# The second matmul of a matmul–GELU–matmul kernel from seven half-size products

## The chip, the cores and the metric

The kernel runs on one core of a Trainium2 chip. The metric is the device time of one execution in microseconds, as a median over several executions. Beside these, one execution was profiled, and its trace gives the start and end of each instruction.

## The reference

```python
m, k, n, p = 1024, 1024, 2048, 1024        # a: m x k, b: k x n, c: n x p, all float32
h = np.matmul(a, b)
h = 0.5 * h * (1 + np.tanh(np.sqrt(2 / np.pi) * (h + 0.044715 * h ** 3)))
return np.matmul(h, c).astype(np.float32)
```

Two matmuls, with a tanh GELU between them. Each has 1024 x 1024 x 2048 multiply-adds.

## The kernel before

The output of the first matmul is kept transposed in SBUF: `hT[h]` holds n on the partitions (16 tiles of 128, the index `t`) and 512 of the 1024 rows of a in the free dimension; `h` is 0 for the upper and 1 for the lower half of a's rows. So the first matmul takes tiles of b as weights and a transposed, `aT[h]` (8 tiles of k), as moving operand; the second takes tiles of `hT[h]` as weights and rows of c as moving operand. All operands of TensorE are bf16. A matmul instruction has 128 x 128 weights and up to 512 moving columns[...]. Six banks rotate in the pool `ppool`, two in `tpool`.

The order of the work is written by hand, and each engine works through its instructions in the order of the program:

1. SP loads the upper half of a and 768 columns of b (six tiles `t`) in pieces by k. VectorE casts a (L91), TensorE transposes it (L94), VectorE copies it out (L95), ScalarE casts b (L97), and TensorE runs six tiles for each k (`mm0`, L86).
2. A small GpSimd copy (L75) waits for a piece of b. Behind it GpSimd issues, in its order, all other loads, which cast float32 to bf16 on the way: 512 columns of b in four DMAs of two k tiles each (L110, called from L115), 768 columns of b in four DMAs of four k tiles (L134), the lower half of a in four blocks of 128 rows (L142), and c in eight DMAs of two row tiles each (L137). The program waits for an older DMA of its eight slots before it issues a new one.
3. TensorE runs tiles 6 to 9 of the upper half k by k (L118), and then tiles 10 to 15 one after another (`mm1`, L127). After each of the tiles 11 to 14 it transposes one block of the lower half of a (`turn`, L149), and VectorE copies that into `aT[1]` (L150).
4. `mm1` runs all 16 tiles of the lower half. ScalarE applies the GELU to each bank (L103).
5. The second matmul: for each of eight row tiles and two halves of the columns, 16 steps add up in one bank (L171), VectorE copies the bank to SBUF (L163), and SP stores it (L164). The last 512 columns are done as two pieces of 256.

Of the kernel before, what the change touches and what calls it, by code (L numbers as in the profile page):

```python
# [8 lines left out]

F32 = mybir.dt.float32  # L10
BF16 = mybir.dt.bfloat16
AF = mybir.ActivationFunctionType
PSUM = bass.MemoryType.PSUM


@with_exitstack
def kernel(ctx, tc, a, b, c, out):
    nc = tc.nc
    M, K = a.shape
    _, N = b.shape  # L20
    _, P = c.shape
    KT = K // 128
    NT = N // 128
    MT = M // 128
    H = 512
    N0 = 6
    W0 = N0 * 128
    N1 = 4
    W1 = N1 * 128

    av = a.rearrange("(mt p) k -> p mt k", p=128)
    bv = b.rearrange("(kt p) n -> p kt n", p=128)
    cv = c.rearrange("(nt p) q -> p nt q", p=128)

    ctx.enter_context(tc.manual_schedule())
    consts = ctx.enter_context(tc.tile_pool(name="consts", bufs=1))
    keep = ctx.enter_context(tc.tile_pool(name="keep", bufs=1))
    astage = ctx.enter_context(tc.tile_pool(name="astage", bufs=4))
    abf = ctx.enter_context(tc.tile_pool(name="abf", bufs=4))
    b0stage = ctx.enter_context(tc.tile_pool(name="b0stage", bufs=8))  # L40
    opool = ctx.enter_context(tc.tile_pool(name="opool", bufs=4))
    ppool = ctx.enter_context(tc.tile_pool(name="ppool", bufs=6, space=PSUM))
    tpool = ctx.enter_context(tc.tile_pool(name="tpool", bufs=2, space=PSUM))

    warm = consts.tile([128, H], BF16, name="warm")
    nc.vector.memset(warm, 0.0)  # L46
    ident = consts.tile([128, 128], BF16, name="ident")
    make_identity(nc, ident)

    aT = [keep.tile([128, KT, H], BF16, name=f"aT{h}") for h in range(2)]  # L50
    b_sb = keep.tile([128, KT, N], BF16, name="b_sb")
    c_sb = keep.tile([128, NT, P], BF16, name="c_sb")
    hT = [keep.tile([128, NT, H], BF16, name=f"hT{h}") for h in range(2)]


    a_st, b_st = {}, {}

    def load_a0(k, n):
        st = astage.tile([128, 4, 256], F32, name="a_st")
        nc.sync.dma_start(out=st[:, :, 0:n * 128], in_=av[:, 0:4, ds(k * 128, n * 128)])  # L60
        for i in range(n):
            a_st[k + i] = st[:, :, ts(i, 128)]

    def load_b0(k):
        st = b0stage.tile([128, W0], F32, name="b0_st")
        nc.sync.dma_start(out=st, in_=bv[:, k, 0:W0])  # L66
        b_st[k] = st

    gate = consts.tile([128, 1], F32, name="gate")
    for k, n in ((0, 1), (1, 1), (2, 2), (4, 2), (6, 2)):  # L70
        load_a0(k, n)
        for i in range(n):
            load_b0(k + i)

    nc.gpsimd.tensor_copy(gate, b_st[5][:, 0:1])  # L75
    g = consts.tile([128, 1], F32, name="g")
    nc.scalar.activation(g, warm[:, 0:1], AF.Gelu_apprx_tanh)
    wps = tpool.tile([128, H], F32, name="pt")
    for _ in range(10):
        nc.tensor.matmul(wps, warm[:, 0:128], warm, start=True, stop=True)  # L80

    ps = [ppool.tile([128, H], F32, name="ps") for _ in range(N0)]

    def mm0(k):
        for t in range(N0):
            nc.tensor.matmul(ps[t], b_sb[:, k, ts(t, 128)], aT[0][:, k, :],  # L86
                             start=(k == 0), stop=(k == KT - 1))

    for k in range(KT):
        ab = abf.tile([128, 4, 128], BF16, name="ab")  # L90
        nc.vector.tensor_copy(ab, a_st[k])  # L91
        pt = tpool.tile([128, H], BF16, name="pt")
        for j in range(4):
            nc.tensor.transpose(pt[:, ts(j, 128)], ab[:, j, :], ident)  # L94
        nc.vector.tensor_copy(aT[0][:, k, :], pt)  # L95
        for i in range(2):
            nc.scalar.activation(b_sb[:, k, ts(i, W0 // 2)], b_st[k][:, ts(i, W0 // 2)], AF.Copy)  # L97
        if k > 0:
            mm0(k - 1)
    mm0(KT - 1)  # L100

    def gelu(t, h, p):
        nc.scalar.activation(hT[h][:, t, :], p, AF.Gelu_apprx_tanh)  # L103

    for t in range(N0):
        gelu(t, 0, ps[t])


    def load_b(k0, kn, n0, w):
        nc.gpsimd.dma_start(out=b_sb[:, k0:k0 + kn, ds(n0, w)], in_=bv[:, k0:k0 + kn, ds(n0, w)])  # L110

    ps = [(tpool if t < 2 else ppool).tile([128, H], F32, name="pt" if t < 2 else "ps")
          for t in range(N1)]
    for k in range(0, KT, 2):
        load_b(k, 2, W0, W1)  # L115
        for i in range(2):
            for t in range(N1):
                nc.tensor.matmul(ps[t], b_sb[:, k + i, ds(W0 + t * 128, 128)], aT[0][:, k + i, :],  # L118
                                 start=(k + i == 0), stop=(k + i == KT - 1))
    for t in range(N1):  # L120
        gelu(N0 + t, 0, ps[t])


    def mm1(t, h):
        p = ppool.tile([128, H], F32, name="ps")
        for k in range(KT):
            nc.tensor.matmul(p, b_sb[:, k, ts(t, 128)], aT[h][:, k, :],  # L127
                             start=(k == 0), stop=(k == KT - 1))
        gelu(t, h, p)

    W2 = 384
    for n0 in range(W0 + W1, N, W2):
        for k in range(0, KT, 4):
            load_b(k, 4, n0, W2)  # L134

    def load_c(t0):
        nc.gpsimd.dma_start(out=c_sb[:, t0:t0 + 2, :], in_=cv[:, t0:t0 + 2, :])  # L137

    a1 = []
    for j in range(4):  # L140
        st = abf.tile([128, K], BF16, name="ab1")
        nc.gpsimd.dma_start(out=st, in_=av[:, 4 + j, :])  # L142
        a1.append(st)

    def turn(j):
        ab = a1[j]
        pt = tpool.tile([128, KT, 128], BF16, name="pt")
        for k in range(KT):
            nc.tensor.transpose(pt[:, k, :], ab[:, ts(k, 128)], ident)  # L149
        nc.vector.tensor_copy(aT[1][:, :, ts(j, 128)], pt)  # L150

    for t in range(N0 + N1, NT):
        mm1(t, 0)
        if NT - 5 <= t < NT - 1:
            turn(t - (NT - 5))
    for t in range(0, NT, 2):
        load_c(t)
    for t in range(NT):
        mm1(t, 1)

    def store(mt, q0, w, p):
        ot = opool.tile([128, H], F32, name="ot")
        nc.vector.tensor_copy(ot[:, 0:w], p)  # L163
        nc.sync.dma_start(out=out[ts(mt, 128), ds(q0, w)], in_=ot[:, 0:w])  # L164

    for mt in range(MT):
        h, j = divmod(mt, 4)
        for q0, w in ((0, 512), (512, 512)) if mt < MT - 1 else ((0, 512), (512, 256), (768, 256)):
            p = ppool.tile([128, w], F32, name="ps", padded_shape=[128, H])
            for t in range(NT):  # L170
                nc.tensor.matmul(p, hT[h][:, t, ts(j, 128)], c_sb[:, t, ds(q0, w)],  # L171
                                 start=(t == 0), stop=(t == NT - 1))
            store(mt, q0, w, p)


# [1 line left out]
_INS = ['a', 'b', 'c']  # L177
# [26 lines left out]
```

## Time and profile before

| | us |
|---|---|
| median of 11 runs | 131.39 |
| lowest and highest run | 130.78, 133.93 |
| the profiled execution, its own time | 132.36 |
| its span in the trace | 130.3 |
| TensorE busy, share of the span | 119.8, 92% |
| VectorE busy | 20.9, 16% |
| ScalarE busy | 27.2, 21% |
| second matmul (L171) in the chain that ended last | 55.31, from 71.60 |

The span goes from the first to the last instruction in the trace. The rest of the profiled execution's time, 2.06 us, lies around it. TensorE's granted clock was 0.996 of full speed. "PE" is TensorE's matmul, "PEld" its weight load, which runs beside matmuls, "DVE" VectorE, "ACT" ScalarE, "POOL" GpSimd and "SP" the engine that issues plain DMAs. An instruction is named by its line, its engine, its operation and its tiles, output first (`ps<-c_sb,hT`). "Idle before" is the time in which the engine stood still just ahead of such an instruction, followed by what ended it. The chain that ended last follows the work back from the last instruction, at each step to what released it.

### The profile page before, as it was taken

Reading aid. Unit: us, or ns where it says so; the run is one execution under the profiler, and the core shown is the slowest. Engines: PE = TensorE matmul, PEld = TensorE weight load, DVE = VectorE, ACT = ScalarE, POOL = GpSimd, SP = SyncE. Lnnn points to the kernel's source line nnn. Section 1 sums busy time; section 2 is a strip of 40 time slices with the busy share of each in tenths; the row PEclk is TensorE's granted clock in tenths of the full one; section 3 lists DMA queues with packets and bytes.
Section 4 is the critical chain, followed back from the end, with each engine's and each line's share of the span. In section 5 each row is a group of like instructions: output and inputs, shape, how many; then the busy total and the mean of one; then the engine's idle time right before and its main releaser. Section 6 shows DMA issues by size and latency. Waiting matters only on the chain.

```text
span 130.3 us, 1431 instructions
## 1 busy us (share of the span) xinstructions
PE 119.8 (92%) x602; PEld 56.4 (43%) x602; DVE 20.9 (16%) x38; ACT 27.2 (21%) x50; POOL 14.6 (11%) x27
## 2 busy tenths in 40 slices
PE   6847899999299999999999999999999999999990
PEld 2324444443156444444444444444444444444570
DVE  0224451000042100000000022222222222221121
ACT  4055556426113233333333100000000000000000
POOL 2000198333452000000000000000000000000000
PEclk9999999999999999999999999999999999999998
DMA  3999999999999999960000022222111122222231
GB/s 109 212 358 377 379 259 153 190 202 206 210 210 210 211 212 210 211 114 2 0 0 5 0 81 81 81 81 80 62 55 63 67 81 81 81 81 81 81 121 40
DMA packets 12196, 17.37 MB, mean 133 GB/s; under 512 B 800, under 2 KB 6688, under 8 KB 12192
## 3 DMA queue, kind: packets, MB, share of 16 engines
q0 software_dynamic: 5952, 7.87, 35.1%
q1 hardware_dynamic: 6240, 9.44, 20.8%
q8 instruction: 4, 0.07, 0.2%
HBM read 20.97 MB, written 4.19 MB: 193 GB/s over the span
## 4 chain that ended last, share of the span: by engine, by line
PE 70%; DMA 17%; SPq 5%; POOL 5%; issue 0%; DVE 0%
PE ps L171 42%; PE ps L127 27%; DMA ab<-in_a_dram 10%; DMA b_st<-in_b_dram 7%; POOL b_sb L110 4%; SPq L66 3%; PE pt L149 2%; SPq L60 1%; DVE ot L163 0%; POOL gate L75 0%
## 5 line engine op out<-in xcount | busy, mean ns | idle before, releaser
L171 PE MATMUL ps<-c_sb,hT 128*128 128x512 bf16 (+1 forms) x272 | 55.5, 367 | 0.0
L171 PEld LDWEIGHTS <-hT 128*128 128x128 bf16 x272 | 26.6, 98 | 28.9
L127 PE MATMUL ps<-aT,b_sb 128*128 128x512 bf16 x176 | 38.9, 379 | 0.0
L127 PEld LDWEIGHTS <-b_sb 128*128 128x128 bf16 x176 | 17.0, 98 | 20.0 <-DMA b_sb<-in_b_dram 0.4
L103 ACT ACTIVATE hT<-ps 128x512 bf16<-128x512 f32 x30 | 17.3, 602 | 29.6 <-PE ps L127 28.4
L163 DVE COPY ot<-ps 128x512 f32<-128x512 f32 (+1 forms) x17 | 11.2, 661 | 73.2 <-PE ps L171 73.2
L86 PE MATMUL ps<-aT,b_sb 128*128 128x512 bf16 x48 | 11.5, 379 | 0.0
L97 ACT ACTIVATE b_sb<-b_st 128x384 bf16<-128x384 f32 x16 | 7.5, 515 | 10.4 <-DMA b_st<-in_b_dram 10.2
L94 PE MATMUL pt<-ident,ab 128*128 128x128 bf16 x32 | 3.4, 232 | 3.6 <-DVE ab L91 3.6
L137 POOL DMA_DIRECT2D c_sb<-in_c_dram x8 | 5.7, 714 | 7.5 <-DMA b_sb<-in_b_dram 5.3
L86 PEld LDWEIGHTS <-b_sb 128*128 128x128 bf16 x48 | 4.4, 98 | 4.0
L150 DVE COPY aT<-pt 128x1024 bf16<-128x1024 bf16 x4 | 2.8, 692 | 20.0 <-PE pt L149 20.0
L110 POOL DMA_DIRECT2D b_sb<-in_b_dram x8 | 6.0, 769 | 0.0
L80 PE MATMUL pt<-warm 128*128 128x512 bf16 x10 | 4.5, 632 | 1.2 <-DVE warm L46 1.2
L94 PEld LDWEIGHTS <-ab 128*128 128x128 bf16 x32 | 2.3, 104 | 6.6 <-DVE ab L91 5.6
L118 PEld LDWEIGHTS <-b_sb 128*128 128x128 bf16 x32 | 3.1, 98 | 3.8
L118 PE MATMUL pt<-aT,b_sb 128*128 128x512 bf16 x16 | 4.8, 379 | 0.0
L118 PE MATMUL ps<-aT,b_sb 128*128 128x512 bf16 x16 | 4.8, 379 | 0.0
L149 PE MATMUL pt<-ident,ab 128*128 128x128 bf16 x32 | 2.5, 219 | 2.3 <-DMA ab<-in_a_dram 2.3
L91 DVE CAST ab<-a_st 128x512 bf16<-128x512 f32 x8 | 3.5, 441 | 6.1 <-DMA a_st<-in_a_dram 6.1
L95 DVE COPY aT<-pt 128x512 bf16<-128x512 bf16 x8 | 3.4, 425 | 6.3 <-PE pt L94 6.3
L149 PEld LDWEIGHTS <-ab 128*128 128x128 bf16 x32 | 2.0, 98 | 3.5 <-DMA ab<-in_a_dram 2.8
(13 smaller groups left out, 7.4 us busy)
## 6 DMA issues: line engine op xcount, KB each, us to landing
c_sb<-in_c_dram POOLq DMA_DIRECT2D x8, 512.0 KB, 16.1
out_dram<-ot SPq DMA_DIRECT2D x15, 256.0 KB, 2.0
b_st<-in_b_dram SPq DMA_DIRECT2D x8, 384.0 KB, 8.3
a_st<-in_a_dram SPq DMA_DIRECT2D x3, 512.0 KB, 8.5
b_sb<-in_b_dram POOLq DMA_DIRECT2D x4, 384.0 KB, 11.0
b_sb<-in_b_dram POOLq DMA_DIRECT2D x4, 256.0 KB, 6.8
ab<-in_a_dram POOLq DMA_DIRECT2D x4, 256.0 KB, 12.8
a_st<-in_a_dram SPq DMA_DIRECT2D x2, 256.0 KB, 4.4
```

What stands on the lines that cost most here:

```text
L80: nc.tensor.matmul(wps, warm[:, 0:128], warm, start=True, stop=True)
L86: nc.tensor.matmul(ps[t], b_sb[:, k, ts(t, 128)], aT[0][:, k, :], start=(k == 0), stop=(k == KT - 1))
L94: nc.tensor.transpose(pt[:, ts(j, 128)], ab[:, j, :], ident)
L97: nc.scalar.activation(b_sb[:, k, ts(i, W0 // 2)], b_st[k][:, ts(i, W0 // 2)], AF.Copy)
L103: nc.scalar.activation(hT[h][:, t, :], p, AF.Gelu_apprx_tanh)
L110: nc.gpsimd.dma_start(out=b_sb[:, k0:k0 + kn, ds(n0, w)], in_=bv[:, k0:k0 + kn, ds(n0, w)])
L118: nc.tensor.matmul(ps[t], b_sb[:, k + i, ds(W0 + t * 128, 128)], aT[0][:, k + i, :], start=(k + i == 0), stop=(k + i == KT - 1))
L127: nc.tensor.matmul(p, b_sb[:, k, ts(t, 128)], aT[h][:, k, :], start=(k == 0), stop=(k == KT - 1))
L137: nc.gpsimd.dma_start(out=c_sb[:, t0:t0 + 2, :], in_=cv[:, t0:t0 + 2, :])
L149: nc.tensor.transpose(pt[:, k, :], ab[:, ts(k, 128)], ident)
L163: nc.vector.tensor_copy(ot[:, 0:w], p)
L171: nc.tensor.matmul(p, hT[h][:, t, ts(j, 128)], c_sb[:, t, ds(q0, w)], start=(t == 0), stop=(t == NT - 1))
```

## The change

The second matmul is cut in halves in all three dimensions: h into h11, h12 (rows of the upper half; n in 0..1023 and 1024..2047), h21 and h22 (rows of the lower half), and c into c11, c12, c21, c22. The four quarters of the output are made from seven products of these halves in place of eight, with sums formed ahead of the products (operand sums) and behind them:

- operand sums: s1 = h21 + h22, s2 = s1 - h11, s3 = h11 - h21, s4 = h12 - s2; t1 = c12 - c11, t2 = c22 - t1, t3 = c22 - c12, t4 = t2 - c21
- products, in TensorE's order: h11·c11; h12·c21 (three of its four row tiles); s2·t2; s3·t3; s1·t1; s4·c22; h22·t4; and last the fourth row tile of h12·c21, in two pieces of 256 columns

h11, h12, c11, c12 and c21 stay in bf16. h21, h22, c22 and all operand sums are float32r (4 bytes), and so five of the products have float32r operands on both sides. All sums run on VectorE (`tensor_tensor`), 44 on operands, and one or two for each product bank, in place of its copies to the output tile; banks of the first product are copied out by ScalarE. GpSimd copies one bank's result aside for the last piece.

c is loaded by quarters, in the order c11, c22, c21, c12, each in two DMAs of four row tiles. Several tiles take the place of others: c12 and then half of s2 that of `aT[0]`, the other half of s2 that of `aT[1]`, t3 and u3 those of the two parts of b, t1 and t2 the staging tiles of the start. The operand sums are written into the program between and behind the tiles of the lower half, in the order t1, t2, then s1 and t3 by turns, s2, s3. s4 stands between the banks of s3·t3, t4 between those of s1·t1.

In the first half the transposes of a's lower half move: block 0 behind tile 13, blocks 1 to 3 behind tile 14, before tile 15. The 512 columns of b for tiles 6 to 9 are loaded in two DMAs of four k tiles in place of four of two.

```diff
-    b_sb = keep.tile([128, KT, N], BF16, name="b_sb")
-    c_sb = keep.tile([128, NT, P], BF16, name="c_sb")
-    hT = [keep.tile([128, NT, H], BF16, name=f"hT{h}") for h in range(2)]
+    b_lo = keep.tile([128, KT, WB], BF16, name="b_lo", tag="B0")
+    b_hi = keep.tile([128, KT, N - WB], BF16, name="b_hi", tag="B1")
+    hq = [[keep.tile([128, NH, H], F32R if h else BF16, name=f"h{h}{g}") for g in range(2)]
+          for h in range(2)]
...
-    for k in range(0, KT, 2):
-        load_b(k, 2, W0, W1)
-        for i in range(2):
+    for k in range(0, KT, 4):
+        load_b(k, 4, W0, W1)
+        for i in range(4):
...
-        if NT - 5 <= t < NT - 1:
-            turn(t - (NT - 5))
-    for t in range(0, NT, 2):
-        load_c(t)
+        if t == NT - 3:
+            turn(0)
+        if t == NT - 2:
+            turn(1)
+            turn(2)
+            turn(3)
...
+    def load_c(dst, r, q):
+        for t in range(0, NH, 4):
+            nc.gpsimd.dma_start(out=dst[:, t:t + 4, :], in_=cv[:, r * NH + t:r * NH + t + 4, ts(q, H)])
+    load_c(c11, 0, 0)
+    load_c(c22, 1, 1)
+    load_c(c21, 1, 0)
+    load_c(c12, 0, 1)
...
     for t in range(NT):
         mm1(t, 1)
+        if 3 <= t < 7:
+            sum_t1(t - 3)
+        if 6 <= t < 10:
+            sum_t2(2 * (t - 6))
+            sum_t2(2 * (t - 6) + 1)
+        if t == WB // 128:
+            t3 = keep.tile([128, NH, H], F32R, name="t3", tag="B0")
+        if t >= NH + 1:
+            sum_s1(t - NH - 1)
+        if WB // 128 <= t < WB // 128 + 4:
+            i = t - WB // 128
+            nc.vector.tensor_tensor(t3[:, ts(i, 2), :], c22[:, ts(i, 2), :], c12[:, ts(i, 2), :], op=SUB)
+    sum_s1(NH - 1)
+    for i in range(4):
+        nc.vector.tensor_tensor(pair(s2, i), s1[:, ts(i, 2), :], h11[:, ts(i, 2), :], op=SUB)
+    for i in range(4):
+        nc.vector.tensor_tensor(h21[:, ts(i, 2), :], h11[:, ts(i, 2), :], h21[:, ts(i, 2), :], op=SUB)
+    s3 = h21
...
+    def prod(p, lhs, rhs, j, q=slice(0, H)):
+        for t in range(NH):
+            nc.tensor.matmul(p, lhs(t)[:, ts(j, 128)], rhs(t)[:, q],
+                             start=(t == 0), stop=(t == NH - 1))
+    def combine(m, q, p, u, op=ADD, swap=False):
+        ot = new_out()
+        nc.vector.tensor_tensor(ot, u if swap else p, p if swap else u, op=op)
+        store(ot, m, q * H)
...
+    for j in R:
+        p = bank()
+        prod(p, whole(h11), whole(c11), j)
+        nc.scalar.activation(u2[j], p, AF.Copy)
+    for j in range(3):
+        p = bank()
+        prod(p, whole(h12), whole(c21), j)
+        combine(j, 0, p, u2[j])
+    last = u2[3]
+    last_keep = opool.tile([128, H], F32, name="lk", bufs=1)
+    nc.gpsimd.tensor_copy(last_keep, last)
+    for j in R:
+        p = bank()
+        prod(p, halves(s2), ones(t2), j)
+        nc.vector.tensor_tensor(u2[j], p, u2[j], op=ADD)
+    for j in R:
+        p = bank()
+        prod(p, whole(s3), whole(t3), j)
+        nc.vector.tensor_tensor(u3[:, j, :], p, u2[j], op=ADD)
+        sum_s4(j)
+    for j in R:
+        p = bank()
+        prod(p, whole(s1), pairs(t1), j)
+        combine(4 + j, 1, p, u3[:, j, :])
+        nc.vector.tensor_tensor(u2[j], p, u2[j], op=ADD)
+        sum_t4(2 * j)
+        sum_t4(2 * j + 1)
+    for j in R:
+        p = bank()
+        prod(p, halves(s2), whole(c22), j)
+        combine(j, 1, p, u2[j])
+    for j in R:
+        p = bank()
+        prod(p, whole(h22), ones(t2), j)
+        combine(4 + j, 0, p, u3[:, j, :], op=SUB, swap=True)
+    for q in range(2):
+        w = H // 2
+        p = bank(w)
+        prod(p, whole(h12), whole(c21), 3, q=ds(q * w, w))
+        ot = new_out()
+        nc.vector.tensor_tensor(ot[:, 0:w], p, last_keep[:, ds(q * w, w)], op=ADD)
+        store(ot, 3, q * w, w)
```

## The prediction

> **What bounds the kernel now.** I read the page first (busy shares, then the chain of work that ended last), then that chain in order of time, then the groups by shape, and last the timelines of GpSimd, TensorE and VectorE around the first half.
>
> ```profile
> PE 119.8 (92%) x602; PEld 56.4 (43%) x602; DVE 20.9 (16%) x38; ACT 27.2 (21%) x50; POOL 14.6 (11%) x27
> ...
> PE ps L171 42%; PE ps L127 27%; DMA ab<-in_a_dram 10%; DMA b_st<-in_b_dram 7%; POOL b_sb L110 4%; SPq L66 3%; PE pt L149 2%; SPq L60 1%; DVE ot L163 0%; POOL gate L75 0%
> ```
>
> TensorE is the bound and VectorE is nearly free. The second matmul (L171) alone is 42% of the chain. In order of time:
>
> ```profile
> 71.60 55.31 PE ps L171 x272
> 126.91 0.02 issue
> 126.93 0.43 DVE ot L163
> ```
>
> From 71.60 to 126.91 TensorE waits for nothing. The 272 steps are 240 of 512 columns and 32 of 256, worth 256 full ones: 55.31 / 256 = 0.216 us each, start to start. [...] The span's last 3.4 us are the final eviction and store.
>
> Weight loads and evictions by shape (columns: number | busy, mean ns | idle before, who ended it):
>
> ```profile
> L171 PEld LDWEIGHTS <-hT 128*128 128x128 bf16 x272 | 26.6, 98 | 28.9
> L163 DVE COPY ot<-ps 128x512 f32<-128x512 f32 x15 | 10.4, 692 | 70.8 <-PE ps L171 70.8
> ```
>
> A bf16 weight load takes 98 ns and lies wholly beside the matmul before it. The only stall of TensorE in the middle is ahead of the first late transposes, 2.3 us for block 0 of a's lower half:
>
> ```profile
> 35.11 0.62 PE L149 MATMUL pt<-ident,ab 128*128 128x128 bf16 x8 [2.31 <-DMA ab<-in_a_dram]
> ```
>
> GpSimd's timeline dates the loads, since each later issue waits for an earlier load's slot:
>
> ```profile
> 21.82 0.60 POOL L142 DMA_DIRECT2D ab<-in_a_dram  x1
> 23.54 0.55 POOL L142 DMA_DIRECT2D ab<-in_a_dram  x1 [1.12 <-DMA b_sb<-in_b_dram]
> 24.83 0.53 POOL L142 DMA_DIRECT2D ab<-in_a_dram  x1 [0.75 <-DMA b_sb<-in_b_dram]
> 26.11 0.53 POOL L142 DMA_DIRECT2D ab<-in_a_dram  x1 [0.74 <-DMA b_sb<-in_b_dram]
> ```
>
> There are eight slots and eight loads of b ahead, so these waits end when b's loads 2, 3 and 4 (two k tiles each, for L118) land: 23.5, 24.8 and 26.1 us. By the same reading the four loads behind them land at 28.3, 30.3, 32.2 and 34.1 (issues of c at 28.27 to 34.10), and a's four blocks at 35.1, 36.7, 37.9 and 39.1. In one-microsecond windows the load of c fades out at 57.3 us:
>
> ```profile
> 56.00:57.00 1.00, 1.00 (x7) 0.41 (x5) 0.00 (x0) 0.60 (x1) 0.00 (x0) 1.00 0.93 174
> 57.00:58.00 1.00, 1.00 (x6) 0.47 (x5) 0.00 (x0) 0.17 (x1) 0.00 (x0) 1.00 0.27 49
> ```
>
> (last column GB/s written; it was 211 until then).
>
> [...] No row of the trace has a 4-byte matmul. [...] The trace shows the bf16 load only. [...] The trace's bf16 stream, 128 x 512 x 2 bytes in 0.216 us, is 607 GB/s[...] and leaves open whether 4 bytes go as fast. [...] The trace's 512-column fp32 eviction takes 692, so I use 692[...].
>
> **The change, part by part.**
>
> *Product steps.* Seven products of 32 steps are 224 full steps in place of 256: 64 in bf16 (h11·c11, h12·c21, the last of them in halves) and 160 in float32r. The built program has one weight load and one matmul for each step[...]. Its step costs at least 0.216 us[...]. Above, there are two ends: the weight load isn't overlapped, +98 ns (the bf16 load's length, as a stand-in)[...]. I take 0.216: [...]a load twice as long as 98 ns still fits beside a 216 ns matmul. So 224 x 0.216 = 48.4 against 55.3: -6.9 us.
>
> *b for L118 in two loads, not four.* The first load now brings k 0 to 3, so it lands when load 2 did, 23.5. L118 began at 22.15. A new stall on the path, +1.4 us; lower end 0 (it lands before 22.15), upper end about 2. The next one (26.1) is needed at 23.55 + 16 x 0.216 = 27.0, in time. GpSimd issues two DMAs fewer ahead of a; the queue behind is full, so no landing moves.
>
> *Late transposes.* L118 ends at 23.55 + 6.9 = 30.45; tiles 10 to 13 (32 steps) end at 37.35, their b having landed by 34.1. Block 0 (35.1) is there: the 2.3 us stall is gone. Transposes 0.45 → 37.8; tile 14 → 39.55; blocks 1 and 2 → 40.45. Block 3 has landed (39.1), but there are two transpose banks, so it waits for block 1's copy: 40.0 + 0.2 + 0.69 = 40.9, → 41.35. Tile 15 → 43.1. Before, tile 15 began at 42.09 and ended at 43.8. Net of both edits: -0.7 us (-2.1 without the new stall). VectorE's copy of block 3 ends near 42.2, ahead of the second half.
>
> *Loads of c.* Same bytes, 2 KB rows for 4 KB, c22 written as 4 bytes; I cost it at nothing, as the queue reads at about 420 GB/s now (211 written as bf16). c12 takes the place of aT[0] and can't be issued before tile 15 ends (43.1); six of eight loads are ahead of it and run to about 54 (39.1 + 6.3 MB at 420), so GpSimd's wait is covered. Only c12 is queued behind it. c12 lands at 57.3.
>
> *Sums on VectorE.* t1, the first sum, needs c12, and all else queues behind it. After 57.3, up to the last t4 that product 7 needs: 18 of 1024 columns (two t1, four each t3, s2, s3, s4) x 1.224 = 22.0, and 43 of 512 (eight t2, eight s1, 19 operations on product banks, eight t4) x 0.692 = 29.8. Sum 51.8, so t4 ends at 109.1 if VectorE never rests. TensorE's second matmul starts at 70.9 (71.6 - 0.7); product 3 at 70.9 + 56 x 0.216 = 83.0, when s2 is ready at 57.3 + 23.3 = 80.6 (26 operations). Product 7 starts at 70.9 + 184 x 0.216 = 110.6. VectorE is ahead by 1.5 to 2.4 us: nothing on the path, but if that cover went, it would cost microsecond for microsecond. In its favour, two operations in a row overlap in the trace:
>
> ```profile
> 11.22 0.42 DVE L95 COPY aT<-pt 128x512 bf16<-128x512 bf16 x1 [0.49 <-PE pt L94]
> 11.56 0.42 DVE L91 CAST ab<-a_st 128x512 bf16<-128x512 f32 x1
> ```
>
> (0.34 apart, 0.42 long), which would give back up to 61 x 0.08 = 4.9 us. ScalarE's four copies (0.60 each, as L103) and GpSimd's copy of the kept bank have idle engines. Banks: product 3's fourth bank waits for the combine behind s3, 0.3 us on the path, my allowance (0 to 1).
>
> *Sum.* 130.3 - 6.9 - 0.7 + 0.3 = 123.0 us span. The profiled execution took 132.36 with 2.06 outside its span: 125.1. The median of the runs is 131.39, 0.9927 of it: **124.1 us**.
>
> **Rivals.**
> - *VectorE becomes the bound.* If an operation costs 80 ns more than its length instead of less, s2 is 2.1 late and t4 4.9, less the 1.5 to 2.4 in hand: +3.0, 127.1 us. For it: 61 operations without rest, many depending on the one before. Against: the overlap above.
> - *The wider load is hidden.* The first load of b lands before 22.15: -1.4, 122.7 us. For it: fewer issues. Against: load 2 landed at 23.5.
> - *float32r is somewhat slower,* +25 ns a step: +4.0, 128.1 us.
> - *Slower than before: the 4-byte weight load isn't hidden.* Place: 160 steps of products 3 to 7. At +98 ns, 15.7 us: 139.7 us[...]. It decides from 7.3 / 160 = 46 ns a step. For it: [...]no 4-byte row in the trace. Against: TensorE's loads are only 98 of each 216 ns.
>
> **How the numbers follow.** Forecast 0.50; VectorE bound 0.17; load hidden 0.11; somewhat slower float32r 0.06 (0.03 faster, 0.02 same, 0.01 slower); weight load exposed 0.16. A measurement tells about 0.3% from no change. Faster 0.81, same 0.02, slower 0.17. The range 121.8 to 128.2 takes in the first three and most of the fourth, 0.82; only the two ends of the float32r price are left out. The likeliest case's own range is 122.7 to 125.6.
>
> **What would show it.** Right: float32r matmuls 0.216 apart; a stall of about 1.4 us ahead of L118's first step, none ahead of block 0's transposes; the second matmul some 48.5 us long; VectorE busy almost without a break from 57 to 109, TensorE hardly waiting for it. Wrong: a float32r spacing over 0.26; TensorE's waits for VectorE adding to over 2 us; c12 landing after 60.

## The result and the profile after

| | before | after |
|---|---|---|
| median, us | 131.73 (47 runs) | 124.83 (12 runs, 124.33 to 125.62) |
| the profiled execution, us | 132.36 | 124.74 |
| its span, us | 130.3 | 123.0 |

The ratio of the runs is 0.950, with a 95% interval of 0.947 to 0.952; it leaves out executions in a slower state, which the kernel before shows in some of its runs, and so it is not the quotient of the two medians. The forecast was 124.1, with a range of 121.8 to 128.2, and a span of 123.0. The span agrees to the tenth, but, as the steps below show, because errors cancelled.

The page of the changed kernel, busy shares and then the chain that ended last:

```profile
PE 115.2 (94%) x562; PEld 67.2 (55%) x562; DVE 65.1 (53%) x94; ACT 29.6 (24%) x54; POOL 21.6 (18%) x26
...
PE ps L246 41%; PE ps L143 31%; DMA a_st<-in_a_dram 12%; PE ps L102 3%; PE ps L134 3%; PE pt L134 3%; PE pt L162 1%; DVE aT L163 1%; PE pt L110 1%; DVE ab L107 0%; SPq L82 0%; DVE ot L316 0%; SPq L76 0%; DVEq L107 0%
```

There are 40 steps fewer on TensorE and three times the work on VectorE, and still VectorE is on the chain with 1% only. The end of the same chain in order of time (start, length, what):

```profile
38.77 0.70 DVE aT L163
...
40.13 29.35 PE ps L143 x136
69.48 50.14 PE ps L246 x232
...
119.64 0.42 DVE ot L316
```

The second matmul starts at 69.48 where it was 71.60, and takes 50.14 us where it was 55.31. These two differences, 2.1 and 5.2, are the whole of the 7.3 us. The 0.70 us of VectorE is the copy of block 1, for whose bank the transposes of block 3 wait. TensorE's timeline shows the second matmul product by product (the chain counts its start 0.16 us behind the first step's own, in the kernel before as here):

```profile
69.32 12.25 PE L246 MATMUL ps<-c,h 128*128 128x512 bf16 x56
81.22 7.62 PE L246 MATMUL ps<-t,s 128*128 128x512 f32 x32
88.67 7.42 PE L246 MATMUL ps<-t,h 128*128 128x512 f32 x32
95.92 7.42 PE L246 MATMUL ps<-t,s 128*128 128x512 f32 x32
103.18 7.42 PE L246 MATMUL ps<-c,s 128*128 128x512 f32 x32
110.43 7.42 PE L246 MATMUL ps<-t,h 128*128 128x512 f32 x32
117.69 1.92 PE L246 MATMUL ps<-c,h 128*128 128x256 bf16 x16
```

No line has an idle time in brackets: TensorE waits for no sum. Take the starts, not the lengths (a bf16 matmul of 512 columns is 379 ns long in the table of groups): from 88.67 to 117.69 are 128 float32r steps, 226.7 ns each, where bf16 steps stand 216 apart. (The first float32r step is recorded at 81.22, though 56 bf16 steps of 216 ns from 69.32 end at 81.42. So I count back from 88.67.) VectorE's timeline has the sums that TensorE needs; the lines are the first sums of t1, then s2, s3 and the combines behind it, and the last sums of t4:

```profile
56.52 2.36 DVE L200 TENSOR_TENSOR t<-c,c 128x1024 fp32r<-128x1024 bf16 x2 [15.66 <-DMA c<-in_c_dram]
...
75.56 4.63 DVE L230 TENSOR_TENSOR s<-s,h 128x1024 fp32r<-128x1024 f32 x4
80.10 4.63 DVE L232 TENSOR_TENSOR h<-h,h 128x1024 fp32r<-128x1024 bf16 x4
84.64 1.89 DVE L269 TENSOR_TENSOR ot<-ps,u 128x512 f32<-128x512 f32 x3
...
106.34 1.29 DVE L239 TENSOR_TENSOR t<-t,c 128x512 fp32r<-128x512 f32 x2
```

By shape, the weight loads of 4-byte and 2-byte operands:

```profile
L246 PEld LDWEIGHTS ps<-t,s 128*128 128x128 f32 x64 | 12.0, 188 | 2.6
...
L246 PEld LDWEIGHTS <-h 128*128 128x128 bf16 x72 | 7.0, 98 | 7.0 <-issue 0.3
```

### The profile page after: what moved, and what is told of

Its sections match the earlier page's. It is cut to its first block, busy times and chain, and to the rows that moved or that the text cites. A ratio compares the mean times of both kernels' runs of the same rounds, so it can differ in the third digit from the quotient of the medians.

```text
span 123.0 us, 1443 instructions
## 1 busy us (share of the span) xinstructions
PE 115.2 (94%) x562; PEld 67.2 (55%) x562; DVE 65.1 (53%) x94; ACT 29.6 (24%) x54; POOL 21.6 (18%) x26
## 4 chain that ended last, share of the span: by engine, by line
PE 82%; DMA 12%; DVE 1%; SPq 1%; issue 0%; DVEq 0%
PE ps L246 41%; PE ps L143 31%; DMA a_st<-in_a_dram 12%; PE ps L102 3%; PE ps L134 3%; PE pt L134 3%; PE pt L162 1%; DVE aT L163 1%; PE pt L110 1%; DVE ab L107 0%; SPq L82 0%; DVE ot L316 0%; SPq L76 0%; DVEq L107 0%
## 5 line engine op out<-in xcount | busy, mean ns | idle before, releaser
L119 ACT ACTIVATE h<-ps 128x512 fp32r<-128x512 f32 (+1 forms) x30 | 17.3, 601 | 27.5 <-PE ps L143 26.3
L143 PE MATMUL ps<-aT,b_hi 128*128 128x512 bf16 x96 | 21.4, 379 | 0.0
L143 PE MATMUL ps<-aT,b_lo 128*128 128x512 bf16 x80 | 17.4, 379 | 0.0
L143 PEld LDWEIGHTS <-b_hi 128*128 128x128 bf16 x96 | 9.3, 98 | 10.8
L246 PE MATMUL ps<-t,s 128*128 128x512 f32 x64 | 15.0, 392 | 0.0
L246 PE MATMUL ps<-t,h 128*128 128x512 f32 x64 | 14.8, 389 | 0.0
L246 PE MATMUL ps<-c,h 128*128 128x512 bf16 (+1 forms) x72 | 14.2, 355 | 0.0
L246 PEld LDWEIGHTS ps<-t,s 128*128 128x128 f32 x64 | 12.0, 188 | 2.6
L246 PEld LDWEIGHTS ps<-t,h 128*128 128x128 f32 x64 | 12.0, 188 | 2.5
L200 DVE TENSOR_TENSOR t<-c,c 128x1024 fp32r<-128x1024 bf16 x4 | 4.7, 1222 | 15.9 <-DMA c<-in_c_dram 15.7
L143 PEld LDWEIGHTS <-b_lo 128*128 128x128 bf16 x80 | 7.8, 98 | 9.4
L102 PE MATMUL ps<-aT,b_lo 128*128 128x512 bf16 x48 | 12.8, 410 | 0.0
L102 PEld LDWEIGHTS <-b_lo 128*128 128x128 bf16 x48 | 4.7, 104 | 4.7 <-issue 1.1
```

The costliest lines, as they stand in the source:

```text
L102: nc.tensor.matmul(ps[t], bt(k, t), aT[0][:, k, :], start=(k == 0), stop=(k == KT - 1))
L119: nc.scalar.activation(hq[h][t // NH][:, t % NH, :], p, AF.Gelu_apprx_tanh)
L143: nc.tensor.matmul(p, bt(k, t), aT[h][:, k, :], start=(k == 0), stop=(k == KT - 1))
L200: nc.vector.tensor_tensor(t1[i], c12[:, ts(i, 2), :], c11[:, ts(i, 2), :], op=SUB)
L246: nc.tensor.matmul(p, lhs(t)[:, ts(j, 128)], rhs(t)[:, q], start=(t == 0), stop=(t == NH - 1))
```

## The experiments

My theory after the result: the late transposes alone took 2.1 us out of the first half, the wide loads of b did nothing, and the seven products took 5.2, which is 6.9 less 160 steps of about 11 ns, the price of float32r. The rivals were that the wide loads made the first half shorter, and that the 11 ns come from something other than the width of the operands.

### Late transposes alone, and with the wide loads

The first edit puts one part of the change, the moved calls of `turn`, into the kernel before.

> The kernel before with the late transposes alone; b for tiles 6 to 9 still in four loads. My theory (the two parts add up, and the late transposes alone made the first half 2.1 us shorter): 2.1 us less than before (ratio 0.984), second matmul starting at 69.4 to 69.6, no wait of TensorE ahead of block 0's transposes. Rival (the two wide loads of b are what made the first half shorter, by leaving GpSimd's queue sooner): under 1 us of gain, block 0 or its bank later than 36.1.

The second adds the two wide calls of `load_b`.

> The kernel before with the late transposes and the two wide loads of b. My theory: the same as with the late transposes alone, within 0.3 us, since the wide load lands just as tile 6 begins; the first matmul of L118's place starts between 22.1 and 22.5. The prediction's step (the wide load lands at 23.5 and stalls TensorE for 1.4 us): 1.4 us longer than with the late transposes alone. Rival (wide loads help): 0.5 us or more shorter.

Measured: 0.985 (0.980 to 0.990) with the transposes alone, and 0.990 (0.985 to 0.995) with the wide loads too. The intervals overlap. The start of tile 6 shifts by up to 0.9 us between executions, so the traces are compared from the first step of tile 6 to the second matmul (its start in the chain):

| | first step of tile 6 | second matmul | between |
|---|---|---|---|
| before | 22.15 | 71.60 | 49.45 |
| late transposes | 21.27 | 68.61 | 47.34 |
| late transposes, wide loads | 21.61 | 68.95 | 47.34 |
| after | 22.14 | 69.48 | 47.34 |

So 2.1 us are the late transposes, and in these executions the wide loads give and take nothing, as my theory had it. Block 3's wait for its bank is in all three with late transposes:

```profile
38.65 0.61 PE L149 MATMUL pt<-ident,ab 128*128 128x128 bf16 x8 [0.34 <-DVE aT L150]
```

(This is with late transposes alone.) What the wide loads do is seen in a window of one microsecond of the kernel before and then of the changed kernel. The columns are the busy time of TensorE, its weight loads, VectorE, ScalarE and GpSimd, the granted clock, the busy share of the DMA engines, and GB/s written.

```profile
21.00:22.00 1.00, 1.00 (x7) 0.46 (x5) 0.00 (x0) 0.73 (x2) 1.00 (x3) 1.00 0.85 131
```

```profile
21.00:22.00 1.00, 1.00 (x7) 0.39 (x4) 0.00 (x0) 0.74 (x2) 0.54 (x1) 1.00 1.21 202
```

With wide loads the queue moves 202 GB/s in this window and in the one before it, with narrow ones 131 and 150. Over all kernels, ten executions with wide loads have 196 to 211 GB/s in the two windows, and three with narrow ones 131 to 196. So narrow loads were slower on the whole, by how much differs from one execution to the next, and what holds them back was not tried.

Nor do narrow loads always land as late as in the kernel before, where GpSimd's second block of a waited for load 2's slot until 23.54. With late transposes alone it followed the first without a wait, at about 21.7:

```profile
20.96 1.26 POOL L142 DMA_DIRECT2D ab<-in_a_dram  x2
```

The wide load comes just in time, not early. In four of the ten executions with wide loads TensorE was held up by one of the two, by 0.2 to 0.6 us in all, as here with bf16 throughout, in its second run below:

```profile
22.68 0.61 PE L134 MATMUL pt<-aT,b_lo 128*128 128x512 bf16 x2 [0.23 <-DMA b_lo<-in_b_dram]
```

### The seven products alone

The edit puts back the early transposes and the four narrow loads in the changed kernel (these two parts of the change, reversed).

> The changed kernel with the first half as before: transposes after tiles 11 to 14, b for tiles 6 to 9 in four loads. My theory (parts add up): 2.1 us more than the changed kernel, 5.0 to 5.3 less than before (ratio about 0.961), second matmul 50.1 us long. Rival (the seven products only fit because the first half ended early, so that VectorE's sums become late or c12 is late): second matmul over 51 us, or waits of TensorE for VectorE of over 1 us.

Measured: 0.954 (0.948 to 0.961), a span of 124.6 against 123.0, and a second matmul of 50.14 us, the same to the last digit:

```profile
34.61 0.62 PE L162 MATMUL pt<-ident,ab 128*128 128x128 bf16 x8 [2.05 <-DMA ab<-in_a_dram]
...
71.10 50.14 PE ps L242 x232
```

TensorE stood still 2.05 us ahead of block 0, where it was 2.31 in the kernel before. From tile 6 (22.04) to the second matmul it took 49.06 us, so 1.7 us more than in the changed kernel and not 2.1; tile 6 began 0.1 us sooner, and the span is 1.6 longer. What the late transposes save depends on when block 0 lands, and that differs between executions. By the runs, the first half's two edits save 1.0% and the seven products 4.6%, and together 5.0%: the parts add up within their intervals. The products don't need the earlier start. VectorE's first sum began at 56.66 here and at 56.52 in the changed kernel, though c12 was asked for 1.6 us later (43.78 in place of 42.15). In the changed kernel the queue still wrote 208 GB/s from 55 to 56 us and 161 in the next; from this I estimate that the loads ahead of c12 decide when it lands.

### bf16 in place of float32r

```diff
-F32R = mybir.dt.float32r
+F32R = mybir.dt.bfloat16
```

> The changed kernel with bf16 in place of float32r everywhere: all operand sums, h21, h22 and c22 are rounded to bf16, so the operands of five products carry fewer digits. My theory (a float32r step costs 226.7 ns for 216.0 because of its 4-byte operands): all steps 216 ns apart, second matmul 48.4 us long, 1.7 us less than the changed kernel; VectorE's sums shorter too, which changes nothing. Rival (the 10.6 ns come from the many operand tiles, from VectorE's and TensorE's traffic in SBUF or from waits on semaphores): steps stay at 222 to 227 ns and the time within 0.5 us of the changed kernel.

Measured: 0.933 (0.928 to 0.939), second matmul 48.38 us, and a step every 216 ns in every product (the first line is of the chain, the others of the timeline):

```profile
69.63 48.38 PE ps L246 x232
...
81.56 7.07 PE L246 MATMUL ps<-t,s 128*128 128x512 bf16 x32
...
102.28 7.07 PE L246 MATMUL ps<-c,s 128*128 128x512 bf16 x32
```

(81.56 to 102.28 is 96 steps of 215.8 ns.) The operand tiles, the sums and the semaphores are the same, so the extra of a float32r step is the type's: 50.14 - 48.38 = 1.76 us, 11 ns for each of 160 steps. VectorE's sums got shorter as well (those of s2, 1024 columns, 1226 to 684 ns; those of t4, 512 columns, 686 to 421), so this edit alone does not exclude that VectorE's traffic in SBUF slows the steps. The changed kernel's own trace speaks against it: in the product from 95.92 VectorE is busy all the time (7.00 of 7.00 us, 96 to 103), in the one from 110.43 two fifths of it (2.38 of 6.00 us, 111 to 117), and the steps are 226.7 ns in both.

### Product 7 in shorter steps

What of a float32r step is slower: the columns, the weight load, or something fixed? The edit does the product h22·t4 in pieces of 256 and then 128 columns.

```diff
-        p = bank()
-        prod(p, whole(h22), ones(t2), j)
-        combine(4 + j, 0, p, u3[:, j, :], op=SUB, swap=True)
+        for q in range(2):
+            w = H // 2
+            p = bank(w)
+            prod(p, whole(h22), ones(t2), j, q=ds(q * w, w))
+            ot = new_out()
+            nc.vector.tensor_tensor(ot[:, 0:w], u3[:, j, ds(q * w, w)], p, op=SUB)
+            store(ot, 4 + j, q * w, w)
```

> The changed kernel with product h22 by t4 done in 64 steps of 256 columns in place of 32 of 512 (same sums, same result), everything else as it was. A float32r step of 512 columns takes 226.7 ns, and its weight load shows as 188 ns. Theory A (the step is paced by the weight load plus about 39 ns that can't lie beside the matmul ahead): steps stay near 227 ns, the product takes 14.5 us for 7.25, total +7.3 us. Theory B (the load is hidden but has to fit, and the extra is a fixed cost): 188 to 195 ns a step, 12.0 to 12.5 us, +4.8 to +5.2. Theory C (the moving columns of 4 bytes pass more slowly): 113 ns a step, 7.3 us, +0.1 us.

```profile
110.07 7.83 PE L246 MATMUL ps<-t,h 128*128 128x256 f32 x64
117.74 1.92 PE L246 MATMUL ps<-c,h 128*128 128x256 bf16 x16
```

64 steps from 110.07 to 117.74, 119.8 ns each; the span is 0.3 us longer, the ratio 0.954 (0.949 to 0.959). Theories A and B fall: a weight load 188 ns long in steps of 119.8 means that its length is not its rate, and that successive loads overlap. C is nearest, but not right either: 119.8 is not half of 226.7. Between 256 and 512 columns a step grows by 0.4176 ns a column, the bf16 rate (215.8 and 109 ns give 0.417; the 109 are from the last line of the bf16 kernel further down: 1.91 us less the 0.27 of the last step's own length, over 15 steps), on top of something fixed. That made theory D, a fixed 10 ns, which shorter steps should show most clearly. The next two kernels use pieces of 128 columns, in float32r and in bf16 (the diff is against the edit above):

```diff
-        for q in range(2):
-            w = H // 2
+        ot = new_out()
+        for q in range(4):
+            w = H // 4
...
-            ot = new_out()
-            nc.vector.tensor_tensor(ot[:, 0:w], u3[:, j, ds(q * w, w)], p, op=SUB)
-            store(ot, 4 + j, q * w, w)
+            nc.vector.tensor_tensor(ot[:, ds(q * w, w)], u3[:, j, ds(q * w, w)], p, op=SUB)
+        store(ot, 4 + j, 0)
```

> The changed kernel with product h22 by t4 in 128 steps of 128 columns (one output tile and one store for each row tile, as before). Steps of 512 and 256 columns took 226.7 and 119.8 ns, a line with 0.4176 ns a column and 12.9 ns a step. Theory D (a float32r step costs a fixed 10 ns more than a bf16 step, and the weight load's 188 ns overlap each other freely): 66 ns a step, the product 8.5 us long. Rival (the weight load of 4-byte operands has a rate of its own, which longer steps hide): 94 ns or more a step, 12 us or more.

> The same pieces of 128 columns, with bf16 in place of float32r everywhere (operand sums, h21, h22 and c22 rounded to bf16). Theory D: bf16 steps of 512 and 256 columns took 216.0 and about 109.3 ns, a line with 0.417 ns a column and 2.5 ns a step, so 56 ns here, 10 ns under the float32r step, the product 7.2 us long. Rival (short steps of either type meet the same floor): equal spacing of both, above 66 ns.

```profile
110.34 14.40 PE L246 MATMUL ps<-t,h 128*128 128x128 f32 x128
124.58 1.92 PE L246 MATMUL ps<-c,h 128*128 128x256 bf16 x16
```

```profile
109.39 7.31 PE L246 MATMUL ps<-t,h 128*128 128x128 bf16 x128
116.54 1.91 PE L246 MATMUL ps<-c,h 128*128 128x256 bf16 x16
```

float32r: 14.24 us for 128 steps, 111.3 ns each, and 131.64 us for the only run. bf16: 7.15 us, 55.9 ns each. So theory D alone fails here, and the rival's number holds at this length: 111 ns, where bf16 takes 56. That the weight load has a rate of its own, which sets this, is not shown. Weight loads are busy all through this product (13.00 of 13.00 us), but so they are through the product in pieces of 256 (6.00 of 6.00), whose steps are longer, 119.8 ns: being busy doesn't mean setting the pace. What fits the three lengths is the larger of 111 ns and the bf16 step plus 11 ns, two constants for three points:

| columns | bf16 step, ns | float32r step, ns | difference |
|---|---|---|---|
| 512 | 215.8 | 226.7 | 11 |
| 256 | 109 | 119.8 | 11 |
| 128 | 55.9 | 111.3 | 55 |

What the fixed 11 ns are, and what the 111, stays open: three lengths of one product don't tell, and weights and columns had 4 bytes together in every run.

### More sums ahead of product 3

```diff
     sum_s1(NH - 1)
+    for i in range(4):
+        nc.vector.tensor_tensor(t3[:, ts(i, 2), :], c22[:, ts(i, 2), :], c12[:, ts(i, 2), :], op=SUB)
```

> The changed kernel with the four sums t3 written twice, the second time between s1 and s2: 4 x 1.14 us more for VectorE ahead of s2, nothing more for TensorE. My theory (s2 was ready 1.0 us before product 3 could begin, and product 3's first four steps need only the first half of s2): TensorE stands still 2.5 to 2.9 us ahead of product 3 and nowhere else, +2.7 us in all. Rival 1 (VectorE is already the bound further on, at t4): more than 3.5 us. Rival 2 (there is more cover than it seems): under 1 us.

Measured: 0.975 (0.969 to 0.981), a span of 126.6, 3.6 us more. The direction was right and the size was not. TensorE's timeline around product 3:

```profile
81.86 0.70 PE L248 MATMUL ps<-t,s 128*128 128x512 f32 x2 [0.29 <-DVE s L232]
...
85.18 4.37 PE L248 MATMUL ps<-t,s 128*128 128x512 f32 x18 [0.40 <-DVE s L232]
90.32 2.11 PE L248 MATMUL ps<-t,s 128*128 128x512 f32 x8 [0.77 <-DVE ot L271]
```

TensorE takes two steps for each quarter of s2, and begins the seventh at 85.18. In the changed kernel it began at 82.78 (26 steps of 226.7 ns ahead of 88.67), so it is 2.4 us late. That is nearly what I expected. The last line is new: the fourth bank of product 3 waits for the combine that stands in VectorE's queue behind s3 and ended at 90.27; without that wait the line would start at 85.18 + 18 x 0.227 = 89.26. Another 1.1 us, and no wait later on. The sum is as large as rival 1 had it, but at another place: t4 is not short.

VectorE's work came 4.9 us later (4.6 for the four sums, and s2's own sums took 4.92 us in place of 4.63), and TensorE lost 3.6. The difference was in hand. In the changed kernel the last quarter of s2 ended at 80.19 for the step at 82.78, and the combine at 85.33 for a bank that began at 86.86 (8 steps ahead of 88.67): VectorE has 2.6 us in hand at s2 and 1.5 at this bank.

### The kept bank copied by ScalarE, and a copy by GpSimd alone

```diff
     load_c(c12, 0, 1)
+    idle = opool.tile([128, H], F32, name="ot")
+    nc.gpsimd.tensor_copy(idle, b_st[7][:, 0:H])
...
-    nc.gpsimd.tensor_copy(last_keep, last)
+    nc.scalar.activation(last_keep, last, AF.Copy)
```

> The changed kernel with the bank that is kept for the last piece copied by ScalarE, not GpSimd; and as a probe, GpSimd copies 512 float32 columns of a staging tile, which nothing uses, at about 44 us, when VectorE is idle. GpSimd's copy took 8.13 us in the changed kernel while VectorE ran sums without a break. My theory: the copy was off the path, so the time stays within 0.3 us; and GpSimd's copy alone takes 1 us or less, since the 8 us were VectorE holding it off. Rival on GpSimd: the copy is slow by itself, 5 to 8 us again. Rival on the path: 0.5 us or more shorter.

Measured: 0.950 (0.944 to 0.956), span 123.1: no difference. GpSimd's copy in the changed kernel, then the probe in this one, then the copy and VectorE's sums around its end in the kernel with more sums:

```profile
77.08 8.13 POOL L286 COPY lk<-u 128x512 f32<-128x512 f32 x1 [33.45 <-ACT u L279]
```

```profile
43.56 0.63 POOL L195 COPY ot<-b_st 128x512 f32<-128x512 f32 x1
```

```profile
77.09 3.55 POOL L288 COPY lk<-u 128x512 f32<-128x512 f32 x1 [33.45 <-ACT u L281]
...
75.55 4.62 DVE L224 TENSOR_TENSOR t<-c,c 128x1024 fp32r<-128x1024 f32 x4
80.20 4.92 DVE L232 TENSOR_TENSOR s<-s,h 128x1024 fp32r<-128x1024 f32 x4
```

Alone it takes 0.63 us. The 8.13 us end at 85.21, just after VectorE's last sum of two operands in SBUF (84.73). With bf16 throughout, where VectorE rests from 75.5 to 78.4, the same copy took 0.61 us. With more sums it ended at 80.64, just after the one gap in VectorE's queue, 0.03 us between 80.17 and 80.20, and the four sums behind the gap took 0.3 us more than in the changed kernel. So the copy is held off by VectorE's sums while they follow each other without a gap; the 0.3 us would fit its holding up VectorE in turn. In the changed kernel nothing waits for it.

### The changed kernel and bf16 side by side

> The changed kernel once more, on the same chip as the run with bf16 throughout, for a direct comparison: 0.950 of the kernel before.

> The changed kernel with bf16 in place of float32r everywhere (operand sums, h21, h22 and c22 rounded to bf16), once more beside the changed kernel: my theory 1.7 us less than that, 0.937 of the kernel before. Rival (the first run's 0.933 was the chip's): 0.945 or more.

Measured on one chip: 0.950 (0.945 to 0.955; 125.16 us) and 0.936 (0.931 to 0.940; 123.16 us). bf16 throughout is the fastest version here, 2.0 us under the changed kernel (their profiled spans are 1.5 apart, 123.2 and 121.7; tile 6 began 0.3 us later in the second, with the late load of b shown above), for operand sums with fewer digits.

## Why the prediction was right, step by step

- **Product steps.** The mechanism was right, and a term of the sum was mis-sized: 160 steps at 0.216. The runs show 0.2267, so the second matmul saved 5.2 us, not 6.9. The working took the weight load for either hidden or exposed; the price lies between, 11 ns in each step. The reason given against the exposed load holds: a load of 188 ns does fit beside a step of 227. That a 4-byte step costs no less than a bf16 one, and its columns no more, was my estimate: no row of the trace before has a 4-byte matmul. The run shows 128 x 512 x 4 bytes in 0.2267 us, 1156 GB/s, where the bf16 stream of the working is 607: twice the bytes in 1.05 times the time. That its load is twice as long as the bf16 one was an estimate as well; the lengths are 188 and 98 ns.
- **b in two loads.** This step failed. It read load 2's landing, 23.5 us, from one execution of the kernel before, 1.4 us behind tile 6's first step, and took that for fixed. The next DMA that needs load 2's slot shows that it isn't: with late transposes alone, and narrow loads still, GpSimd issued it without a wait at about 21.7, 0.4 us behind tile 6's first step (21.27). In the changed kernel only a weight load waited, for 0.2 us, and tile 6 began at 22.14. The rival "the wider load is hidden", given 0.11, is what happened in the profiled execution; in four of the ten executions with wide loads there was a stall, but of 0.2 to 0.6 us only.
- **Late transposes.** Without the stall the working gave the end of tile 15 as 41.7, and the trace has 41.69. Block 3's wait for its bank was foreseen: 0.34 us.
- **Loads of c.** GpSimd waited 5.8 us for TensorE to free aT[0], as foreseen with nothing behind it but c12, whose first half was there at 56.5. The second half was not there at 57.3: VectorE's third sum waited 0.24 us and began at 59.11. The working took the time at which the writing fades for the landing; in the kernel before too, 16 GB/s were still written between 58 and 59 us. It cost TensorE nothing.
- **Sums on VectorE.** Right in the main. The sums take 689 and 1222 ns, for 692 and 1224 in the working, but stand 0.60 and 1.14 us apart, the overlap that was seen between two copies. (The trace before has no float32 operation of VectorE on 1024 columns; a line through its evictions of 256 and 512 columns, 425 and 692 ns, gives 1226.) s2 was ready at 80.2 (forecast 80.6) and t4 at 107.6 (109.1). Product 3 began at about 81.4, not 83.0, since the first half ended 1.4 us sooner than forecast, so the cover at s2 was 1.2 us by the working's measure, not 2.4. That measure is too strict, as product 3 reads the last quarter of s2 only in its seventh step: 2.6 us were in hand.
- **The bank behind s3.** 0.3 us were allowed and none was needed; the experiment with more sums shows that it has less in hand than s2, 1.5 us.
- **The sum.** -6.9 became -5.2, -0.7 became -2.1, and +0.3 became 0: -7.3 in both cases. That the span came out to the tenth is luck: three terms were off, by 1.7, -1.4 and -0.3 us.
- **From span to median.** The sum was scaled by 0.9927, the place of one profiled execution among eleven runs. The working's time for the profiled execution itself was 125.1, and it took 124.74, since 1.7 us lay outside its span and not 2.06. The scaling took off another 0.9 us, which the changed kernel's runs don't show: their median, 124.83, lies 0.1 above the profiled execution. So the scaling made the forecast of the median 0.7 us too low; without it, it would have been 0.2 too high.

## What to carry to other kernels

Fewer matmul steps are worth their steps only if the sums run beside other work: here 44 sums took VectorE from 16% to 53% busy and cost TensorE nothing, with 1.5 us in hand at the tightest place that was found, because they began as soon as the first half of c's last quarter had landed. Price a step from starts, not from lengths, and an operand type at the length of step that is used: float32r cost 5% at 512 columns (226.7 ns for 215.8) and doubled the step at 128 (111.3 for 55.9). When a stall seems to move from one place to another, compare from a common event, as the start of this kernel shifts by up to 0.9 us, and the effects sought were 0.4 to 2.1.

## What the runs showed of the hardware that was not expected

- A float32r step costs 11 ns more than a bf16 step at 512 and 256 columns, and takes 111 ns at 128, where bf16 takes 56.
- VectorE's sums over two SBUF operands overlap by about 0.09 us when they follow each other: 512 columns are 689 ns long and 0.60 us apart. The forecast had seen such an overlap between two copies and not counted on it.
- GpSimd's copy of 512 float32 columns grew from 0.63 to 8.13 us beside such sums. Sums back to back held it off: in the changed kernel it ended at 85.21, just after the last of them (84.73), and in the kernel with more sums it came through at a gap of 0.03 us.
